# Gate and up projection in three 256-column passes, stationary operands moved by 64 bytes

## The chip, the cores and the metric

The kernel runs on one core of a Trainium2 chip. The metric is the device time of one execution in microseconds, given as the median of several runs. A profiled execution is taken besides; its trace has the start and the length of each engine's instructions.

## The reference

A trunk of two pre-norm layers over 256 tokens of width 1024, all in float32. Layer 0 mixes tokens by attention with a forget gate, layer 1 by block-sparse attention with a relative-position bias; with 256 tokens the one block of layer 1 is the whole sequence, so it is plain causal attention with a bias. Each layer ends with a SwiGLU feed-forward part and a gated embedding:

```python
def reference(...):
    h = x
    for i in range(DEPTH):                       # DEPTH = 2
        u = _rmsnorm(h, attn_norm_g[i])
        proj = u @ w_in                          # q, k, v (layer 0: and the forget gates)
        h = h + _merge_heads(attention(q, k, v)) @ w_o
        u = _rmsnorm(h, ffn_norm_g[i])
        gu = u @ ffn_w_in[i]                     # D_FF = 2816 columns of gate, 2816 of up
        h = h + (jax.nn.silu(gu[..., :D_FF]) * gu[..., D_FF:]) @ ffn_w_out[i]
        gate = jax.nn.sigmoid(_rmsnorm(h, ple_norm_g[i]) @ ple_w_gate[i])
        h = h + gate * (p[i] @ ple_w_up[i])
    return _rmsnorm(h, final_norm_g)
```

## The kernel before

**Split products.** Every matrix product is made of three products of split operands, so that it comes near float32. An operand is written as a high part (`hi`, rounded to TensorE's float32r) and a low part (`lo`, what is left). `mm3` (line 72) accumulates hi*hi, hi*lo and lo*hi in PSUM. In a call `mm(o, a, b)` the operand `a` is stationary: TensorE loads it as weights of 128 columns, a LDWEIGHTS in the profile, before each matmul. The operand `b` is moving: its columns stream through, up to 512 in a pass.

**Weights.** The host packs all weights into tiles of 128 x 1024 in the order of use. `half()` (line 106) fetches the next one by SP's queue into `raw`, ScalarE copies it into `whi` (line 119), and VectorE subtracts to give `wlo` (line 120). There are six buffers of each. `blocks()` (line 123) is the same tile seen as eight stationary blocks of 128 columns.

**Where weights move and where they stand still.** In the products of v, the output projection wo, the down projection fo, the gate pg and the embedding pu, the tokens are stationary and 512 columns of weights move (`tokens`, line 221). In the query and key projections pq (`project`, line 356) the weights are stationary, 128 columns for one block of features, and the 256 tokens move; the norm's result `g` is held in eight blocks of hi and lo, 256 columns each and next to each other (`Norm.both`, line 133). In the attention's values po (`values`, line 418) slices of `vhi` and `vlo` are stationary and the 256 columns of transposed probabilities move. `vhi` and `vlo` are tiles of 128 x 8 x 192 (line 211).

**Gate and up.** `up` (line 466) makes one block of 128 features of gate (a = 0) and of up (a = 1) for each `f` of 22. Here the kernel uses two passes for the three products: `whi` against hi and lo side by side, 512 columns into one whole bank (line 473), then `wlo` against hi, 256 columns, added to the bank's left half (line 475). The bank's right half so holds hi*lo. `gated` (line 497) copies the right half out on ScalarE (line 502), adds the left half on VectorE (503), multiplies by the row of norm factors (504), takes SiLU on ScalarE and the product with up on VectorE, and splits the result for the down projection `fo`. The first two blocks (`f` = 0 and 1) are interleaved by `k`, since the norm's second half is transposed in their midst; from then on each round makes two blocks of gate and up, then 24 passes of `fo` for the two blocks before.

**Order.** Each engine runs its instructions in the program's order. PSUM has eight banks; one pool of eight tiles rotates over them. Buffers are released by semaphores that the tile framework sets. In the built program all operands of matmuls begin at a multiple of 256 bytes in their partition, but for three kinds: the 16-column weights of the forget gate (`fh` and `fl`, 64 bytes apart), the bias table (`rl`), and the broadcast columns `col`.

Of the kernel before, what the change touches and what calls it, by code (L numbers as in the profile page):

```python
# [28 lines left out]
F32R = mybir.dt.float32r  # L29
AF = mybir.ActivationFunctionType  # L30
ALU = mybir.AluOpType

P = 128
S = 256
D = 1024
KT = D // P
H = 16
DH = 64
NP = H // 2
# [7 lines left out]
HW = 1024  # L47
# [4 lines left out]
RVW = 384  # L52


@with_exitstack
def trunk(ctx: ExitStack, tc: tile.TileContext, x, xt, pt, w, wf, cst, gains, gf, bf, rel, hot, rvm, out):
    nc = tc.nc
    one = ctx.enter_context(tc.tile_pool(name="one", bufs=1))
    work = ctx.enter_context(tc.tile_pool(name="work", bufs=2))
# [4 lines left out]
    def bank(name):  # L64
        return ps.tile([P, 512], F32, tag="bank", name=name)

    def f32(ap):
        return ap.bitcast(F32)

    mm = nc.tensor.matmul  # L70

    def mm3(o, a, b, start, stop):
        (ah, al), (bh, bl) = a, b
        mm(o, ah, bh, start=start, stop=False, skip_group_check=True)  # L74
        mm(o, ah, bl, start=False, stop=False, skip_group_check=True)  # L75
        mm(o, al, bh, start=False, stop=stop, skip_group_check=True)  # L76
# [26 lines left out]

    state = {"next": 0}

    def half():

        i = state["next"]
        state["next"] += 1
        raw = work.tile([P, HW], F32, tag="raw", bufs=RAW, name=f"raw{i}")  # L110
        hi = work.tile([P, HW], F32R, tag="whi", bufs=6, name=f"whi{i}")
        lo = work.tile([P, HW], F32R, tag="wlo", bufs=6, name=f"wlo{i}")
        parts = 2 if i < 2 else 1
        for q in range(parts):
            c = slice(q * HW // parts, (q + 1) * HW // parts)
            if i == 0 and q == 1:
                nc.sync.dma_start(hx[:, 1], xt[:, 1])
            nc.sync.dma_start(raw[:, c], w[i][:, c])
            nc.scalar.activation(hi[:, c], raw[:, c], AF.Copy)  # L119
            nc.vector.tensor_tensor(lo[:, c], raw[:, c], f32(hi[:, c]), op=ALU.subtract)  # L120
        return hi, lo

    def blocks():

        return [t.rearrange("p (k c) -> p k c", k=KT) for t in half()]


    class Norm:
# [51 lines left out]

    nm = Norm(0)
    first = [half()]
    nm.block(0, hx[:, 0])
    nm.block(1, hx[:, 1])
    first.append(half())
    for b in range(1, 4):
        nc.sync.dma_start(hx[:, 2 * b:2 * b + 2], xt[:, 2 * b:2 * b + 2])
# [20 lines left out]
    nc.gpsimd.memset(nhalf, -0.5)  # L208
    zero = one.tile([H, S], F32, name="zero")
    nc.gpsimd.memset(zero, 0.0)  # L210
    vhi = one.tile([P, NP, 192], F32R, name="vhi")
    vlo = one.tile([P, NP, 192], F32R, name="vlo")
    vf = one.tile([P, NP, 192], F32, name="vf")
    for t in (f32(vhi), f32(vlo), vf):
        nc.gpsimd.memset(t[:, :, DH:2 * DH], 0.0)
# [1 line left out]
    def split(hi, lo, src):  # L217
        nc.scalar.activation(hi, src, AF.Copy)
        nc.vector.tensor_tensor(lo, src, f32(hi), op=ALU.subtract)

    def tokens(o, x, t, w, start, stop):

        at = slice(t * P, (t + 1) * P)
        mm3(o, (x[0][:, at], x[1][:, at]), w, start, stop)
# [10 lines left out]
    def residual(hf, bks):  # L235
        for t in range(2):
            at = h[:, t, hf * HC:(hf + 1) * HC]
            nc.vector.tensor_tensor(at, at, bks[t], op=ALU.add)
# [67 lines left out]
    def attention(layer, nm, mid, early, nf):  # L306
# [49 lines left out]
        def project(j, a):  # L356
            hi, lo = blocks()
            if a == 0:
                pq[j] = bank(f"pq{layer}_{j}")
            bk = pq[j]  # L360
            for k in range(KT):
                mm3(bk[:, a * S:(a + 1) * S], (hi[:, k], lo[:, k]), nm.k(k),
                    start=(k == 0), stop=(k == KT - 1))
            if a == 0:
                return
            del pq[j]
            t = work.tile([P, 2, S], F32, tag="qkt", name=f"qkt{layer}_{j}")
            nc.vector.tensor_tensor(t.rearrange("p a s -> p (a s)"), bk,
                                    nm.row.rearrange("p a s -> p (a s)"), op=ALU.mult)
            th = work.tile([P, 2, S], F32R, tag="qkh", name=f"qkh{layer}_{j}")  # L370
            tl = work.tile([P, 2, S], F32R, tag="qkl", name=f"qkl{layer}_{j}")
            split(th, tl, t)
            qk[j] = t, th, tl
# [88 lines left out]
    def ffn(layer, nm, filler, np_):  # L462
        acc = []
        prod = {}

        def up(fs):

            bks = {(f, a): bank(f"gu{layer}_{f}_{a}") for f in fs for a in range(2)}

            def step(f, a, wt, k):  # L470
                hi, lo = wt
                b = bks[f, a]
                mm(b, hi[:, k], nm.both[:, k].rearrange("p a s -> p (a s)"), start=(k == 0), stop=False,  # L473
                   skip_group_check=True)
                mm(b[:, 0:S], lo[:, k], nm.hi[:, k], start=False, stop=(k == KT - 1), skip_group_check=True)  # L475

            if fs[0] == 0:
                wts = {f: (blocks(), blocks()) for f in fs}
                for k in range(KT):
                    if k == 3:  # L480
                        nm.turn(1)
                        nm.square(1)
                    for f in fs:
                        for a in range(2):
                            step(f, a, wts[f][a], k)
                nm.root()
                return fs, bks
            for a in range(2):
                wt = blocks()
                for k in range(KT):  # L490
                    step(fs[0], a, wt, k)
                if fs[0] == 2 and a == 0:
                    nm.spread()
                    gated(*early)
            gated(fs, bks)

        def gated(fs, bks):
            for f in fs:
                t = work.tile([P, 2, S], F32, tag="t2k", bufs=3, name=f"gut{layer}_{f}")
                for a in range(2):  # L500
                    b = bks[f, a]
                    nc.scalar.activation(t[:, a], b[:, S:2 * S], AF.Copy)  # L502
                    nc.vector.tensor_tensor(t[:, a], t[:, a], b[:, 0:S], op=ALU.add)  # L503
                nc.vector.tensor_tensor(t, t, nm.row, op=ALU.mult)  # L504
                sg = work.tile([P, S], F32, tag="sg", name=f"sg{layer}_{f}")
                nc.scalar.activation(sg, t[:, 0], AF.Silu)
                nc.vector.tensor_tensor(sg, sg, t[:, 1], op=ALU.mult)
                th = work.tile([P, S], F32R, tag="th", bufs=4, name=f"fh{layer}_{f}")
                tl = work.tile([P, S], F32R, tag="tl", bufs=4, name=f"fl{layer}_{f}")
                split(th, tl, sg)  # L510
                prod[f] = th, tl

        def down(f, wt):
            hi, lo = wt
            for t in range(2):
                for hf in range(2):
                    cols = slice(hf * HC, (hf + 1) * HC)
                    tokens(acc[hf][t], prod[f], t, (hi[:, cols], lo[:, cols]), f == 0, False)

        def last(f, hf):  # L520

            wt = half()
            for i in range(2):
                for t in range(2):
                    tokens(acc[hf][t], prod[f + i], t, [w[:, i * HC:(i + 1) * HC] for w in wt],
                           False, f + i == FT - 1)

        early = up([0, 1])
        acc.extend([bank(f"fo{layer}_{hf}_{t}") for t in range(2)] for hf in range(2))
        for f in range(2, FT, 2):  # L530
            up([f])
            up([f + 1])
            if f == FT - 6:
                pp = filler()
            if f < FT - 2:
                down(f - 2, half())
                down(f - 1, half())
        last(FT - 4, 0)
        filler(pp)
        last(FT - 2, 0)  # L540
        residual(0, acc[0])
        last(FT - 4, 1)
        np_.turn(0)
        np_.square(0)
        last(FT - 2, 1)
        residual(1, acc[1])
# [83 lines left out]
    for layer in range(2):  # L630
# [8 lines left out]
        nm = Norm(3) if layer == 0 else None  # L639
# [95 lines left out]
```

## Time and profile before

| | |
|---|---|
| median of 3 runs | 684.88 us (684.73 to 684.99) |
| the profiled execution's own time | 686.33 us |
| its span, first to last instruction | 684.6 us |
| mean granted TensorE clock | 0.993 |

How to read the profile: PE is TensorE's matmuls and PEld its weight loads; they overlap. DVE is VectorE, ACT ScalarE, POOL GpSimd. A row of a group has line, engine, operation, output<-inputs, shapes and count, then busy time in us and the mean of one in ns, then the engine's idle time before them and what ended it. A row of the timeline has the start in us, the length in us, the engine, line, operation and shape, and how many in a row were merged. A matmul's length includes the time to drain the array, which overlaps the next matmul, so the distance of two starts is what a pass costs. The chain is the work that ended last, followed back from the end. The profile calls all operands f32 or fp32r by their width.

### The profile page before, as it was taken

The numbers are of one execution on the slowest core, as the hardware profiler recorded it, in microseconds if no ns is written. First come the engines' busy times: TensorE is split into PE (matmuls) and PEld (weight loads), VectorE is DVE, ScalarE is ACT, GpSimd is POOL, SyncE is SP. The second block draws the span as 40 slices with busy tenths as digits, with TensorE's granted clock in tenths as the row PEclk, the third lists the DMA queues.
The fourth block names the chain that finished last, engine by engine and source line by source line (L and its number), as shares of the span: only waits on it lengthen the run. The fifth ranks groups of instructions, "written<-read, shape, count | busy, mean of one in ns | idle before, by whom it ended". The sixth has DMA issues, their size and how long they took to land.

```text
span 684.6 us, 10549 instructions
## 1 busy us (share of the span) xinstructions
PE 668.7 (98%) x3876; PEld 580.1 (85%) x3876; DVE 478.4 (70%) x868; ACT 411.2 (60%) x786; POOL 29.4 (4%) x55
## 2 busy tenths in 40 slices
PE   8999999999999999999999999999999999999994
PEld 6798998888888888888889999888888888888883
DVE  4688886678666666766676788766866666676673
ACT  6876665575555555557665766656655555555663
POOL 1066000000000000000000000000000000000000
PEclk9999999999999999999999999999999999999998
DMA  7989333446655555555586533343665555565401
GB/s 267 376 287 350 124 124 124 154 150 225 190 195 189 189 186 199 186 185 185 182 282 197 168 125 124 110 168 109 238 209 184 184 185 189 185 208 191 164 1 62
DMA packets 37524, 125.81 MB, mean 184 GB/s; under 512 B 4240, under 2 KB 7008, under 8 KB 37472
## 3 DMA queue, kind: packets, MB, share of 16 engines
q1 hardware_dynamic: 36016, 121.35, 52.5%
q0 software_dynamic: 608, 2.11, 0.9%
q10 hardware_dynamic: 848, 1.68, 0.7%
q8 instruction: 30, 0.49, 0.3%
q14 instruction: 22, 0.18, 0.1%
HBM read 124.03 MB, written 4.24 MB: 187 GB/s over the span
## 4 chain that ended last, share of the span: by engine, by line
PE 94%; DMA 2%; ACT 1%; issue 1%; DVE 1%; SPq 0%; POOLq 0%; POOL 0%; DVEq 0%; ACTq 0%
PE gu L473 24%; PE gu L475 12%; PE fo L74 6%; PE fo L76 6%; PE fo L75 6%; PE pq L74 5%; PE pq L75 5%; PE pq L76 5%; PE wo L76 2%; PE wo L74 2%; PE wo L75 2%; PE pg L76 2%; PE pg L74 2%; PE pg L75 2%; PE pp L410 2%; PE v L76 2%
## 5 line engine op out<-in xcount | busy, mean ns | idle before, releaser
L120 DVE TENSOR_TENSOR wlo<-raw,whi 128x1024 fp32r<-128x1024 f32 (+1 forms) x218 | 264.8, 1218 | 169.2 <-ACT whi L119 167.8
L119 ACT ACTIVATE whi<-raw 128x1024 fp32r<-128x1024 f32 (+1 forms) x218 | 228.4, 1051 | 195.3 <-issue 67.6
L473 PE MATMUL gu<-g,whi 128*128 128x512 f32 x704 | 249.4, 398 | 0.0
L475 PE MATMUL gu<-g,wlo 128*128 128x256 f32 x704 | 197.5, 281 | 0.0
L473 PEld LDWEIGHTS gu<-g,whi 128*128 128x128 f32 x704 | 132.2, 188 | 32.4
L475 PEld LDWEIGHTS gu<-g,wlo 128*128 128x128 f32 x704 | 132.9, 189 | 0.7
L74 PE MATMUL pq<-g,whi 128*128 128x256 f32 x256 | 75.3, 294 | 0.0
L75 PE MATMUL pq<-g,whi 128*128 128x256 f32 x256 | 73.0, 285 | 0.0
L76 PE MATMUL pq<-g,wlo 128*128 128x256 f32 x256 | 72.9, 285 | 0.0
L74 PE MATMUL fo<-whi,fh 128*128 128x512 f32 x176 | 69.3, 394 | 0.0
L76 PE MATMUL fo<-whi,fl 128*128 128x512 f32 x176 | 68.8, 391 | 0.0
L75 PE MATMUL fo<-wlo,fh 128*128 128x512 f32 x176 | 68.6, 390 | 0.0
L74 PEld LDWEIGHTS pq<-g,whi 128*128 128x128 f32 x256 | 49.7, 194 | 0.9 <-ACT whi L119 0.6
L75 PEld LDWEIGHTS pq<-g,whi 128*128 128x128 f32 x256 | 49.7, 194 | 0.0
L76 PEld LDWEIGHTS pq<-g,wlo 128*128 128x128 f32 x256 | 49.6, 194 | 0.0
L76 PEld LDWEIGHTS fo<-whi,fl 128*128 128x128 f32 x176 | 33.0, 188 | 7.5
L74 PEld LDWEIGHTS fo<-whi,fh 128*128 128x128 f32 x176 | 33.0, 188 | 7.1
L75 PEld LDWEIGHTS fo<-wlo,fh 128*128 128x128 f32 x176 | 33.1, 188 | 6.3
L503 DVE TENSOR_TENSOR gut<-gut,gu 128x256 f32<-128x256 f32 x88 | 36.1, 416 | 0.5 <-ACT gut L502 0.5
L502 ACT ACTIVATE gut<-gu 128x256 f32<-128x256 f32 x88 | 31.8, 369 | 0.0
L394 ACT ACTIVATE e<-e,mn 128x128 f32<-128x128 f32 x64 | 28.3, 444 | 5.7 <-DVE mn L391 5.5
L504 DVE TENSOR_TENSOR gut<-gut,row 128x512 f32<-128x512 f32 x44 | 30.2, 691 | 1.2
(134 smaller groups left out, 909.2 us busy)
## 6 DMA issues: line engine op xcount, KB each, us to landing
raw<-w SPq DMA_DIRECT2D x214, 512.0 KB, 3.3
d<-d SPq DMA_DIRECT2D x4, 768.0 KB, 12.8
bias<-cd POOLq DMA_DIRECT2D x4, 512.0 KB, 8.7
bias<-d SPq DMA_DIRECT2D x4, 512.0 KB, 6.2
raw<-w SPq DMA_DIRECT2D x4, 256.0 KB, 5.3
h<-x ACTq DMA_DIRECT2D x2, 512.0 KB, 5.7
hx<-xt SPq DMA_DIRECT2D x3, 256.0 KB, 5.8
p<-pt SPq DMA_DIRECT2D x2, 256.0 KB, 3.8
```

What stands on the lines that cost most here:

```text
L74: mm(o, ah, bh, start=start, stop=False, skip_group_check=True)
L75: mm(o, ah, bl, start=False, stop=False, skip_group_check=True)
L76: mm(o, al, bh, start=False, stop=stop, skip_group_check=True)
L119: nc.scalar.activation(hi[:, c], raw[:, c], AF.Copy)
L120: nc.vector.tensor_tensor(lo[:, c], raw[:, c], f32(hi[:, c]), op=ALU.subtract)
L394: nc.scalar.activation(e[:, sl[q]], e[:, sl[q]], AF.Exp, scale=-1.0, bias=mn[:, q:q + 1], accum_out=mn[:, 2 + q:3 + q])
L410: nc.tensor.transpose(pp[:, q * P:(q + 1) * P], e[:, q * P:(q + 1) * P], ident)
L473: mm(b, hi[:, k], nm.both[:, k].rearrange("p a s -> p (a s)"), start=(k == 0), stop=False, skip_group_check=True)
L475: mm(b[:, 0:S], lo[:, k], nm.hi[:, k], start=False, stop=(k == KT - 1), skip_group_check=True)
L502: nc.scalar.activation(t[:, a], b[:, S:2 * S], AF.Copy)
L503: nc.vector.tensor_tensor(t[:, a], t[:, a], b[:, 0:S], op=ALU.add)
L504: nc.vector.tensor_tensor(t, t, nm.row, op=ALU.mult)
```

## The change

Stationary weights (pq, gate and up) and v now begin 64 bytes past a multiple of 256 bytes; the tiles are 256 bytes longer for it. Weights that move stay at a multiple of 256. Gate and up are made by `mm3`, three passes of 256 columns, into the left and the right half of one bank, and `gated` multiplies the bank by the row factors at once.

```diff
+LINE = 64
+APART = 16
...
-    def half():
+    def half(at=0):
...
-        hi = work.tile([P, HW], F32R, tag="whi", bufs=6, name=f"whi{i}")
-        lo = work.tile([P, HW], F32R, tag="wlo", bufs=6, name=f"wlo{i}")
+        hi, lo = (work.tile([P, HW + LINE], F32R, tag=n, bufs=6, name=f"{n}{i}")[:, at:at + HW] for n in ("whi", "wlo"))
...
-        return [t.rearrange("p (k c) -> p k c", k=KT) for t in half()]
+        return [t.rearrange("p (k c) -> p k c", k=KT) for t in half(APART)]
...
-    vhi = one.tile([P, NP, 192], F32R, name="vhi")
-    vlo = one.tile([P, NP, 192], F32R, name="vlo")
+    vhi, vlo = (one.tile([P, NP * 192 + LINE], F32R, name=n)[:, APART:APART + NP * 192].rearrange("p (j c) -> p j c", j=NP)
+                for n in ("vhi", "vlo"))
...
-            bks = {(f, a): bank(f"gu{layer}_{f}_{a}") for f in fs for a in range(2)}
-
-            def step(f, a, wt, k):
-                hi, lo = wt
-                b = bks[f, a]
-                mm(b, hi[:, k], nm.both[:, k].rearrange("p a s -> p (a s)"), start=(k == 0), stop=False,
-                   skip_group_check=True)
-                mm(b[:, 0:S], lo[:, k], nm.hi[:, k], start=False, stop=(k == KT - 1), skip_group_check=True)
+            bks = {f: bank(f"gu{layer}_{f}") for f in fs}
+
+            def step(f, a, wt, k, start):
+                mm3(bks[f][:, a * S:(a + 1) * S], (wt[0][:, k], wt[1][:, k]), nm.k(k), start, k == KT - 1)
...
-                            step(f, a, wts[f][a], k)
+                            step(f, a, wts[f][a], k, k == 0 and a == 0)
...
-                    step(fs[0], a, wt, k)
+                    step(fs[0], a, wt, k, k == 0)
...
-                for a in range(2):
-                    b = bks[f, a]
-                    nc.scalar.activation(t[:, a], b[:, S:2 * S], AF.Copy)
-                    nc.vector.tensor_tensor(t[:, a], t[:, a], b[:, 0:S], op=ALU.add)
-                nc.vector.tensor_tensor(t, t, nm.row, op=ALU.mult)
+                nc.vector.tensor_tensor(t.rearrange("p a s -> p (a s)"), bks[f],
+                                        nm.row.rearrange("p a s -> p (a s)"), op=ALU.mult)
```

## The prediction

> **What bounds the kernel now.** I read the page first: busy shares, the granted clock and the chain that ended last.
>
> ```profile
> span 684.6 us, 10549 instructions
> ...
> PE 668.7 (98%) x3876; PEld 580.1 (85%) x3876; DVE 478.4 (70%) x868; ACT 411.2 (60%) x786; POOL 29.4 (4%) x55
> ...
> PEclk9999999999999999999999999999999999999998
> ...
> PE 94%; DMA 2%; ACT 1%; issue 1%; DVE 1%; SPq 0%; POOLq 0%; POOL 0%; DVEq 0%; ACTq 0%
> PE gu L473 24%; PE gu L475 12%; PE fo L74 6%; PE fo L76 6%; PE fo L75 6%; PE pq L74 5%; PE pq L75 5%; PE pq L76 5%; PE wo L76 2%; PE wo L74 2%; PE wo L75 2%; PE pg L76 2%; PE pg L74 2%; PE pg L75 2%; PE pp L410 2%; PE v L76 2%
> ```
>
> TensorE makes 94% of the chain at the full clock, so only the spacing of its passes counts. The busy time of a matmul overlaps the next one; I therefore take spacings from start times in the timeline. The groups give the counts:
>
> ```profile
> L473 PE MATMUL gu<-g,whi 128*128 128x512 f32 x704 | 249.4, 398 | 0.0
> L475 PE MATMUL gu<-g,wlo 128*128 128x256 f32 x704 | 197.5, 281 | 0.0
> L74 PE MATMUL pq<-g,whi 128*128 128x256 f32 x256 | 75.3, 294 | 0.0
> L74 PE MATMUL po<-th,vhi 128*128 128x256 f32 x32 | 9.3, 289 | 0.0
> ```
>
> Query/key projections (pq) are 3 x 256 = 768 passes of 256 columns, the values (po) 3 x 32 = 96 more. One undisturbed stretch of pq, first and last of 24 passes:
>
> ```profile
> 47.86 0.28 PE L74 MATMUL pq<-g,whi 128*128 128x256 f32 x1
> ...
> 50.62 0.28 PE L76 MATMUL pq<-g,wlo 128*128 128x256 f32 x1
> ```
>
> 2.76 us over 23 steps: 120 ns a pass. The down projection (fo), 512 columns a pass, 12 steps:
>
> ```profile
> 206.43 0.39 PE L74 MATMUL fo<-whi,fh 128*128 128x512 f32 x1
> ...
> 209.15 0.39 PE L473 MATMUL gu<-g,whi 128*128 128x512 f32 x1
> ```
>
> 2.72 / 12 = 226.7 ns. The 256 extra columns cost 106.7 ns, so 256 columns alone are worth 106.7 ns, and each pass carries **13.3 ns that its columns don't explain**. Gate and up (gu) alternate a pass of 512 and one of 256:
>
> ```profile
> 209.15 0.39 PE L473 MATMUL gu<-g,whi 128*128 128x512 f32 x1
> 209.38 0.28 PE L475 MATMUL gu<-g,wlo 128*128 128x256 f32 x1
> 209.49 0.40 PE L473 MATMUL gu<-g,whi 128*128 128x512 f32 x1
> 209.72 0.28 PE L475 MATMUL gu<-g,wlo 128*128 128x256 f32 x1
> 209.84 0.40 PE L473 MATMUL gu<-g,whi 128*128 128x512 f32 x1
> 210.08 0.28 PE L475 MATMUL gu<-g,wlo 128*128 128x256 f32 x1
> 210.20 0.40 PE L473 MATMUL gu<-g,whi 128*128 128x512 f32 x1
> ...
> 220.44 0.40 PE L74 MATMUL fo<-whi,fh 128*128 128x512 f32 x1
> ```
>
> 32 pairs in 11.29 us: 352.8 ns a pair, 16.4 ns over the columns' 320.0 for each of its two passes. The starts repeat every three pairs (1.05 to 1.06 us) and not every pair. Yet the same instructions hold another rhythm earlier, 16 pairs in 5.55 us, 346.9 ns:
>
> ```profile
> 147.74 0.39 PE L473 MATMUL gu<-g,whi 128*128 128x512 f32 x1
> ...
> 153.29 0.39 PE L74 MATMUL fo<-whi,fh 128*128 128x512 f32 x1
> ```
>
> 704 x 352.8 = 248.4 us for gu, which is the 36% that the chain gives it.
>
> **What the excess is.** After a stall of PE the granted clock fell for about 3 us (the 0.98 of the stage from 35 us in the table further down), and ten pq passes ran so:
>
> ```profile
> 54.71 0.41 PE L76 MATMUL pq<-g,wlo 128*128 128x256 f32 x1
> ...
> 56.84 0.41 PE L74 MATMUL pq<-g,whi 128*128 128x256 f32 x1
> ```
>
> 213 ns a pass is twice 106.7, so the clock was at half, with nothing left over. A dead time fixed in ns would still be there, and one fixed in array cycles would have doubled. So the excess looks like two streams getting in each other's way at full rate: a pass's moving columns, and the load of the next pass's weights, which starts with it:
>
> ```profile
> 47.86 0.19 PEld L75 LDWEIGHTS pq<-g,whi 128*128 128x128 f32 x1
> ```
>
> That gu has two rhythms for the same work says the loss depends on how the two streams fall against each other. In the program every operand of these passes starts on a multiple of 256 bytes, so both streams start at the same place in the line; that is what the change shifts. Against it speaks the forget-gate product pf, whose weights are 16 columns and start 0, 64, 128 and 192 bytes into the line in turn:
>
> ```profile
> 20.86 0.28 PE L74 MATMUL pf<-g,fh 128*16 128x256 f32 x1
> ...
> 23.20 0.28 PE L76 MATMUL pf<-g,fl 128*16 128x256 f32 x1
> ```
>
> 2.34 us over 20 steps: 117 ns throughout, with no step that follows the offset. But those loads read one 64-byte piece, against eight, and the passes sit below the 120.
>
> The floor of a weight load of 128 columns shows where the moving side is short, in eight transposes (128 columns each):
>
> ```profile
> 133.75 1.03 PE L148 MATMUL tp<-ident,h 128*128 128x128 f32 x8
> ...
> L148 PE MATMUL tp<-ident,h 128*128 128x128 f32 x80 | 10.4, 272 | 0.0
> ```
>
> (1.03 - 0.27) / 7 = 109 ns from one to the next. No pass with new weights can be expected under that.
>
> **The change part by part.** *The shift of stationary operands.* It touches the weights of gu and pq and the v operands of po. fo, wo, pg and v keep their places, so their 226.7 ns stays. Call the new spacing of a 256-column pass X. No row shows a full load shifted against its moving operand. Its lower bound is the load's 109. For the upper, two streams that stay in step hold 120; a gu pass of 512 shows more, up to 0.24 us (209.84 to 210.08), 26.7 ns over its columns, hence 133. I take **X = 112**, nearest to the 256-column steps of 0.11 to 0.12 in the gu rows (209.38 to 209.49), a little over the floor. 864 passes x (120 - 112) = 6.9 us gained; at 109, 9.5; at 120, nothing; at 133, 11.2 lost.
>
> *Gate and up in three 256-column passes.* 704 pairs become 2,112 passes, with one weight load more a pair. New cost 704 x 3 x 112 = 236.5 us against 248.4: 11.9 us gained; at 109 it is 230.2 (18.2 gained); at 120 it is 253.4 (5.0 lost); at 133 it is 280.9 (32.5 lost). Note that by itself this edit loses at today's spacing.
>
> *One bank and a shorter gate.* Removed: a copy and an addition for each half. The row product now reads the bank, for which qkt is the nearest row:
>
> ```profile
> L502 ACT ACTIVATE gut<-gu 128x256 f32<-128x256 f32 x88 | 31.8, 369 | 0.0
> L503 DVE TENSOR_TENSOR gut<-gut,gu 128x256 f32<-128x256 f32 x88 | 36.1, 416 | 0.5 <-ACT gut L502 0.5
> L504 DVE TENSOR_TENSOR gut<-gut,row 128x512 f32<-128x512 f32 x44 | 30.2, 691 | 1.2
> L368 DVE TENSOR_TENSOR qkt<-pq,row 128x512 f32<-128x512 f32 x16 | 10.8, 677 | 2.5 <-PE pq L76 2.5
> ```
>
> ScalarE loses 31.8 us, VectorE 36.1 + 44 x 0.014 = 36.7. PE waited for neither (its idle is 0.0 in the gu rows), so this is worth 0 on the path: TensorE's own queue hides it. It would be worth something only if VectorE came to bind. The instruction order on each engine is otherwise that of before, with gu blocks of 48 passes where 32 stood; no DMA is added or moved.
>
> *Can the feeders keep up?* By stage:
>
> ```profile
> 35.00:106.00 71.00, 69.50 (x576) 66.36 (x576) 59.01 (x158) 47.98 (x126) 22.20 (x37) 0.98 0.61 215
> 165.00:310.00 145.00, 145.00 (x759) 123.45 (x758) 100.44 (x142) 77.20 (x125) 0.00 (x0) 1.00 0.58 193
> 369.00:436.00 67.00, 67.00 (x573) 64.22 (x573) 53.52 (x154) 46.23 (x121) 0.00 (x0) 1.00 0.44 141
> ```
>
> Columns after the length are PE, PEld, DVE, ACT, POOL, clock, DMA share, GB/s. Attention has some 430 of the 864 passes per layer, so it shrinks by 3.5 us: VectorE goes from 59.0 of 71 to 59.0 of 67.5 (87%) in layer 0, where it already made PE wait once for 1.5 us. In the feed-forward stretch it gets lighter, and 193 GB/s rises by a few per cent, under the 215 of the first attention. I take nothing off; the range holds a microsecond or two of stall.
>
> *Sum.* 6.9 + 11.9 = 18.8 us. The profiled execution took 686.33 us for a span of 684.60 (1.73 around it), hence 667.5 for such an execution; the three unprofiled runs have a median of 684.88, 1.45 lower, hence **666**.
>
> The Trainium skill gives a warm gap of N/2.4 + 2.5 ns (TensorE: Matmul & The Clock Gate, Back-to-back issue gap); for 256 columns that is 109.2 ns, by which the sum would be 27 us gained, 658. The measured 120 and 226.7 lie 11 ns above it.
>
> **The rivals.** *The shift does nothing* (the other side). The 13.3 ns belongs to the exchange of weights, not to addresses. Then X stays 120, the pairs go from 352.8 to 360, and the time is 684.88 + 5.0 = **690**. For it: pf's 117 at four offsets. Against it: the half-clock passes without excess, and two rhythms for one instruction sequence. It decides from X = (248.4 + 103.7) us / 2,976 passes = 118.3 ns on: any smaller relief loses. The same page (What happens when you issue a matmul) speaks for this rival: "Loading the next tile's weights doesn't steal SBUF read bandwidth from the running matmul." By that rule no offset can help; the trace agrees as far as pf goes and disagrees in the half-clock passes.
>
> *The shift hurts.* The load of 512 bytes now touches three 256-byte stretches instead of two, or the streams lock one step worse: X = 127 to 133, 2,976 x (127 - 118.3) = 26 us or more lost, **711** and up. Nothing in the profile speaks for it but the 26.7 ns of single gu passes.
>
> *A part of it goes.* The passes move to pf's 117: 704 x (352.8 - 351) + 864 x 3 = 3.9 us gained, **681**.
>
> *All of it goes.* X = 109: 27.7 us gained, **657**.
>
> **How the numbers follow.** Forecast with X from 109 to 115: 0.52, its own range 657 to 675. Partial relief: 0.08. Break-even within 0.2% (1.4 us, about what a measurement here can tell from none): 0.04. Nothing: 0.27. Harm: 0.09. Faster is 0.52 + 0.08 = 0.60, same 0.04, slower 0.36. The range reaches from full relief, 657, to the first rival with a little stall, 692; harm is left out.
>
> **What would show it.** Right: pq and gu passes 110 to 115 ns apart in the timeline, gu blocks of 96 passes in some 10.8 us where 11.29 stood, fo unchanged at 226.7, and VectorE's idle in gu longer. Wrong: pq still at 120 (the shift is nothing), weight loads or passes beyond 125 (harm), or PE idle before sp with VectorE as the releaser (the feeder binds).

## The result, and the profile after

The changed kernel takes **683.58 us** (median of 20 runs, 682.1 to 685.1) against 684.91 us for the kernel before (20 runs, 684.31 to 687.71): a ratio of 0.9974, 95% interval 0.9966 to 0.9983. It is faster, as forecast, but by 1.3 us (1.8 by the ratio) and not by 18.8; the time lies inside the range of 657 to 692 and far from the 666 that stood in it.

The page of the changed kernel, its busy shares, the clock and the groups of gate and up:

```profile
span 682.0 us, 11771 instructions
...
PE 666.4 (98%) x4580; PEld 611.0 (90%) x4580; DVE 452.5 (66%) x780; ACT 385.9 (57%) x698; POOL 29.1 (4%) x55
...
PEclk9998999999999999999999999999999999999997
...
L78 PE MATMUL gu<-g,whi 128*128 128x256 f32 x704 | 198.2, 281 | 0.0
L80 PE MATMUL gu<-g,wlo 128*128 128x256 f32 x704 | 197.8, 281 | 0.0
L79 PE MATMUL gu<-g,whi 128*128 128x256 f32 x704 | 197.8, 281 | 0.0
...
L499 DVE TENSOR_TENSOR gut<-gu,row 128x512 f32<-128x512 f32 x44 | 30.0, 689 | 18.0 <-PE gu L80 18.0
```

TensorE is as full as before, at the same mean clock (0.992 against 0.993); the 704 added passes are there. VectorE (478.4 to 452.5 us) and ScalarE (411.2 to 385.9 us) have become lighter, and VectorE now waits 18.0 us for gate and up: the relief shows up as waiting, as it must on an engine that doesn't set the end.

Where the 1.3 us came from is read by the starts of stages. Timeline rows of the kernel before (first pass of gu and of pg in layer 0, of pq and of wo in layer 1):

```profile
129.52 0.40 PE L473 MATMUL gu<-g,whi 128*128 128x512 f32 x1
...
321.68 0.39 PE L74 MATMUL pg<-whi,g 128*128 128x512 f32 x1
...
368.31 0.36 PE L74 MATMUL pq<-g,whi 128*128 128x256 f32 x1
...
432.57 0.47 PE L74 MATMUL wo<-whi,o 128*128 128x512 f32 x1
```

and the same four of the changed kernel:

```profile
128.12 0.28 PE L78 MATMUL gu<-g,whi 128*128 128x256 f32 x1
...
320.25 0.39 PE L78 MATMUL pg<-whi,g 128*128 128x512 f32 x1
...
366.88 0.37 PE L78 MATMUL pq<-g,whi 128*128 128x256 f32 x1
...
430.04 0.47 PE L78 MATMUL wo<-whi,o 128*128 128x512 f32 x1
```

The feed-forward stage took 192.16 us and takes 192.13: **gate and up gave nothing**. Layer 1's attention took 64.26 us and takes 63.16: 1.1 us came from there. Layer 0's attention, with the fall of the clock in it, took 67.38 us and takes 66.80 (from the first pq pass at 35.29 and 34.52 to the first wo pass at 102.67 and 101.32). One round of gu and fo shows why. Timeline of the changed kernel, the first pass of 96 of gu, then of 24 of fo, then the next round:

```profile
157.51 0.28 PE L78 MATMUL gu<-g,whi 128*128 128x256 f32 x1
...
168.82 0.40 PE L78 MATMUL fo<-whi,fh 128*128 128x512 f32 x1
...
174.29 0.28 PE L78 MATMUL gu<-g,whi 128*128 128x256 f32 x1
```

11.31 us over 96 passes is **117.8 ns a pass**, where 32 pairs took 11.29 us before; all 18 rounds between two blocks of fo are alike. The query and key projections show two spacings. Rows of the changed kernel, an early block of 24 passes (first and last), and 23 passes of a late one:

```profile
47.00 0.28 PE L78 MATMUL pq<-g,whi 128*128 128x256 f32 x1
...
49.61 0.28 PE L80 MATMUL pq<-g,wlo 128*128 128x256 f32 x1
...
92.47 0.28 PE L79 MATMUL pq<-g,whi 128*128 128x256 f32 x1
...
95.06 0.28 PE L80 MATMUL pq<-g,wlo 128*128 128x256 f32 x1
```

2.61 / 23 = 113.5 ns, and 2.59 / 22 = 117.7 ns: the same instruction, the same offset, two rhythms, neither of them the 120 of before.

### The profile page after: what moved, and what is told of

Read it like the earlier page. It is cut to its first block, busy times and chain, and to the rows that moved or that the text cites. A ratio compares the mean times of both kernels' runs of the same rounds, so it can differ in the third digit from the quotient of the medians.

```text
span 682.0 us, 11771 instructions
## 1 busy us (share of the span) xinstructions
PE 666.4 (98%) x4580; PEld 611.0 (90%) x4580; DVE 452.5 (66%) x780; ACT 385.9 (57%) x698; POOL 29.1 (4%) x55
## 4 chain that ended last, share of the span: by engine, by line
PE 90%; issue 1%; DVE 0%; ACT 0%; POOLq 0%; POOL 0%; ACTq 0%
PE gu L80 12%; PE gu L78 12%; PE gu L79 12%; PE fo L78 6%; PE fo L79 6%; PE fo L80 6%; PE pq L78 4%; PE pq L79 4%; PE pq L80 4%; PE wo L78 2%; PE wo L80 2%; PE wo L79 2%; PE pg L80 2%; PE pg L78 2%; PE pg L79 2%; PE pp L413 2%
## 5 line engine op out<-in xcount | busy, mean ns | idle before, releaser
L78 PE MATMUL gu<-g,whi 128*128 128x256 f32 x704 | 198.2, 281 | 0.0
L79 PE MATMUL gu<-g,whi 128*128 128x256 f32 x704 | 197.8, 281 | 0.0
L79 PEld LDWEIGHTS gu<-g,whi 128*128 128x128 f32 x704 | 134.7, 191 | 0.7
L78 PEld LDWEIGHTS gu<-g,whi 128*128 128x128 f32 x704 | 132.4, 188 | 0.8
L78 PE MATMUL pq<-g,whi 128*128 128x256 f32 x256 | 74.5, 291 | 0.0
L79 PE MATMUL pq<-g,whi 128*128 128x256 f32 x256 | 72.2, 282 | 0.0
L221 ACT ACTIVATE fh<-sg 128x256 fp32r<-128x256 f32 x44 | 18.1, 415 | 47.5 <-DVE sg L503 47.5
L499 DVE TENSOR_TENSOR gut<-gu,row 128x512 f32<-128x512 f32 x44 | 30.0, 689 | 18.0 <-PE gu L80 18.0
```

Source lines behind the costliest of these rows:

```text
L499: nc.vector.tensor_tensor(t.rearrange("p a s -> p (a s)"), bks[f], nm.row.rearrange("p a s -> p (a s)"), op=ALU.mult)
```

## The experiments

Two questions were open: is it the offset that moves the spacing, and why 117.8 in one place and 113 in another. Each kernel is compared with the kernel before, which ran beside it on the same chip. From chip to chip the median of the kernel before went from 684.91 to 685.45 us, so a difference between two of the experiments, or between one and the changed kernel's 683.58, is good to about half a microsecond.

### The shift alone

The 64 bytes, with gate and up left in passes of 512 and 256 columns.

```diff
-        return [t.rearrange("p (k c) -> p k c", k=KT) for t in half()]
+        return [t.rearrange("p (k c) -> p k c", k=KT) for t in half(APART)]
```

> The kernel before with the 64-byte shift of stationary weights and v alone; gate and up keep their pairs of 512 and 256 columns in two banks. Theory A (the shift eases a contention whose size depends on how the load of weights falls against the moving columns): pq passes 113 to 118 ns apart as in the changed kernel, 864 passes x 2 to 6 ns = 2 to 5 us gained there; the gu pairs go from 352.8 ns to about 348, another 3 us gained; about 678 to 681 us. Theory B (the shift does nothing, and the gain of the changed kernel is from the passes or from the lighter gate): pq at 120 ns, pairs at 352.8 ns, 684.9 us. Theory C (the shift is of use to passes of 256 columns alone): pq 113 to 118, pairs still 352.8 ns, 680 to 683 us.

685.08 us (12 runs) against 685.45; ratio 0.9987 (0.9974 to 1.0). The timeline of this kernel, 16 pairs of gu up to fo:

```profile
163.80 0.40 PE L476 MATMUL gu<-g,whi 128*128 128x512 f32 x1
...
169.45 0.40 PE L78 MATMUL fo<-whi,fh 128*128 128x512 f32 x1
```

5.65 / 16 = 353.1 ns a pair, as before (352.8). A pair of 512 and 256 columns gains nothing from the 64 bytes. The passes of pq did move: layer 1's attention took 63.24 us in this trace, where 64.26 stood. But each feed-forward stage took 0.2 us more (192.37 against 192.16). So the spacings are those of theory C, and the time is not: it is theory B's 684.9.

### The passes alone

The changed kernel with the distance set back to 0.

```diff
-APART = 16
+APART = 0
```

> The changed kernel without the shift: all stationary operands at a multiple of 256 bytes, gate and up in three passes of 256 columns into one bank. Theory A: gu and pq passes stay in step at 120 ns, gu costs 704 x 360 = 253.4 us against 248.4, about 690 us. Theory B: as the changed kernel, passes of 118 ns and about 683.6 us.

689.09 us (6 runs, 688.81 to 690.05) against 685.45; ratio 1.0045 (1.0029 to 1.0061). The timeline of this kernel, first of 96 passes of gu and the first of fo:

```profile
157.28 0.28 PE L78 MATMUL gu<-g,whi 128*128 128x256 f32 x1
...
168.79 0.40 PE L78 MATMUL fo<-whi,fh 128*128 128x512 f32 x1
```

11.51 / 96 = 119.9 ns. Against the kernel before it this is 3.6 us lost, where the first rival of the prediction said 5. The changed kernel gained 1.3, so with the three passes the shift is worth 3.64 + 1.33 = 5.0 us. At 64 bytes neither half of the change gains by itself (the shift alone 0.4 us, its interval reaching to none); together they come out a little ahead.

### TensorE alone, many offsets

A kernel with only TensorE working: stationary and moving operands lie in SBUF, runs of 48 passes of 256 columns cycle through them at a given distance, behind six passes of 512 columns (`a`) or behind transposes (`b`). The trunk is left out, and x is returned.

```diff
+    def narrow(name, off, cols, n=48, moff=0):
+        for i in range(n):
+            w = stt[:, 1 if j == 2 else 0, o + k * 128:o + k * 128 + cols]
+            mm(b[:cols, 0:S], w, mvt[:, c:c + S], start=(i == 0), stop=(i == n - 1), skip_group_check=True)
```

> TensorE alone, on operands that are loaded once; the trunk is left out and x is returned. Runs of 48 passes of 256 columns with 128 stationary columns that begin 0, 16, 32, 48, 64, 96, 128, 160, 192 and 224 bytes past a multiple of 256, each entered three ways (behind passes of 512 columns, behind four transposes, behind a product of two 128-column passes); then passes of 512 columns at 0, 64 and 128, loads of 16, 32 and 64 columns, and moving operands shifted by 64 and 128 bytes. Theory A: 120 ns at 0, 113 to 118 at 64, and a spacing that changes with the offset and with the entry; 512 columns go from 226.7 to about 220 when shifted. Theory B: 120 ns at every offset. If VectorE, ScalarE and the DMAs of the kernel make the excess (theory D), every run here comes near 109.

The timeline of this kernel. `n64a` has the stationary operand 64 bytes off, `w` rows have 512 columns a pass, `c16` and `c32` have 16 and 32 stationary columns at offset 0, `m64u0` has the moving operand alone 64 bytes off, and `m64u64` both:

```profile
18.11 5.92 PE L55 MATMUL n0a<-mv,stt 128*128 128x256 f32 x48
...
82.28 6.14 PE L55 MATMUL n48b<-mv,stt 128*128 128x256 f32 x48
...
95.73 5.82 PE L55 MATMUL n64a<-mv,stt 128*128 128x256 f32 x48
...
101.74 5.71 PE L55 MATMUL n64b<-mv,stt 128*128 128x256 f32 x48
...
192.08 5.77 PE L55 MATMUL n224a<-mv,stt 128*128 128x256 f32 x48
...
209.78 5.61 PE L62 MATMUL w0y<-mv,stt 128*128 128x512 f32 x24
215.23 5.76 PE L62 MATMUL w64y<-mv,stt 128*128 128x512 f32 x24
...
227.76 5.76 PE L55 MATMUL c16u0z<-mv,stt 128*16 128x256 f32 x48
...
234.75 5.61 PE L55 MATMUL c32u0z<-mv,stt 128*32 128x256 f32 x48
...
255.51 5.82 PE L55 MATMUL m64u0a<-mv,stt 128*128 128x256 f32 x48
...
268.65 5.91 PE L55 MATMUL m64u64a<-mv,stt 128*128 128x256 f32 x48
```

The spacing is (length - 0.28) / 47, for 512 columns (length - 0.39) / 23. At offset 0 it is 120.0 ns; at 64 bytes 117.9 behind passes of 512 columns. Behind transposes the first step takes some 0.2 us, and the other 46 average (5.71 - 0.28 - 0.20) / 46 = 113.7. At 224 bytes it is 116.8, and at 48 bytes behind transposes (6.14 - 0.28 - 0.20) / 46 = 123.0. With both operands moved it is back at 119.8, and with the moving operand alone moved by 64 bytes it is 117.9, as with the weights at 192 (117.8): only their distance within 256 bytes counts. For 512 columns 0 is better: 227.0 against 233.5. All this is with the other engines idle (VectorE is busy for 0.1 us of this kernel's span, ScalarE for 7.2 at its start): gate, memory traffic and PSUM readers have no part in it. Theory A's 220 ns for shifted passes of 512 columns did not come. With 32 stationary columns the spacing at offset 0 is 113.4, with 16 it is 116.6, against 120.0 with 128: the length of the weight load counts too, but the shortest is not the fastest.

### One transpose ahead of each round

If the way a run of passes is entered picks its rhythm, something between fo and gu should move it.

```diff
+            if fs[0] % 2 == 0:
+                nc.tensor.transpose(bks[fs[0]][:, 0:P], ident, ident)
```

> The changed kernel with one transpose of the identity (128 columns, overwritten at once) ahead of each round of gate and up. In the changed kernel pq passes run 113.3 ns apart in some stretches and 117.8 in others, gu always 117.8; in the run with TensorE alone a shift of 64 bytes gave 117.8 behind 512-column passes and 113.3 behind transposes. Theory A (two rhythms for the same passes, and how the run is entered picks one): gu passes at 113.3 ns, 22 rounds x (96 x 4.5 - 110) ns = 7 us gained on the changed kernel, about 677 us. Rival (gu's 117.8 comes from what goes on beside it, DMA and VectorE work of the feed-forward stage, and the entry is of no matter): gu stays at 117.8 and the transposes cost 22 x 0.11 = 2.4 us, about 686 us.

682.49 us (6 runs) against 685.37; ratio 0.9956 (0.9939 to 0.9973). Two rounds in this kernel's timeline, each from the second pass of gu to the first of fo:

```profile
173.82 0.28 PE L79 MATMUL gu<-g,whi 128*128 128x256 f32 x1
...
184.60 0.40 PE L78 MATMUL fo<-whi,fh 128*128 128x512 f32 x1
...
190.31 0.28 PE L79 MATMUL gu<-g,whi 128*128 128x256 f32 x1
...
201.50 0.40 PE L78 MATMUL fo<-whi,fh 128*128 128x512 f32 x1
```

10.78 / 95 = 113.5 ns in the one, 11.19 / 95 = 117.8 in the other, with the same instructions and the same entry. Of the 18 rounds behind fo 8 ran at 113.5 and 10 at 117.8, in the same order in both layers: the entry matters, but one transpose does not settle it.

### Entries compared, more offsets

TensorE alone again: at 64 bytes with different single passes as the entry (behind 512-column passes each time), and finer offsets.

```diff
+        wide(f"w{i}z", 0, 6)
+        one_pass(f"b{i}z", *arg)
+        narrow(f"e{i}z", 64, 128)
```

> TensorE alone, trunk left out. Passes of 256 columns at offsets 8, 56, 72, 80, 88, 112, 144, 176, 208 and 240 bytes, entered from 512-column passes and from one transpose; passes of 512 columns at 16, 32, 48, 96, 160, 192, 208, 224 and 240; and at 64 bytes nine ways of entry (one or two transposes, one pass of other sizes), then 24 passes of 512 columns and 24 passes of 256 again. Theory A: spacings between 113 and 123 that depend on offset and entry; 512 columns nowhere under 226.7 or only a little, as 0 was the best of 0, 64 and 128; at 64 bytes one transpose gives 113.3 like four, and the 512-column passes in between throw it back to 117.8. Rival (spacing set by the offset alone): the nine entries all give one value.

The timeline of this kernel: 88 bytes behind 512-column passes and behind one transpose; then 64 bytes behind one transpose (`e0z`), behind two (`e1z`), and behind one pass of 256 columns whose stationary operand is at offset 0 (`e7z`); then 24 passes at 64 bytes after 24 passes of 512 columns at offset 0 (`g7z`); last, 64 bytes behind one pass of 512 columns that is itself at 64 bytes (`e8z`):

```profile
68.17 5.63 PE L55 MATMUL n88a<-mv,stt 128*128 128x256 f32 x48
...
73.67 5.85 PE L55 MATMUL n88b<-mv,stt 128*128 128x256 f32 x48
...
196.35 5.71 PE L55 MATMUL e0z<-mv,stt 128*128 128x256 f32 x48
...
211.73 5.90 PE L55 MATMUL e1z<-mv,stt 128*128 128x256 f32 x48
...
303.90 5.60 PE L55 MATMUL e7z<-mv,stt 128*128 128x256 f32 x48
...
314.81 2.99 PE L55 MATMUL g7z<-mv,stt 128*128 128x256 f32 x24
...
319.26 5.61 PE L55 MATMUL e8z<-mv,stt 128*128 128x256 f32 x48
```

`e7z` holds (5.60 - 0.28) / 47 = 113.2 from its first step. `e0z` reaches it after a few steps, `e1z` stays at (5.90 - 0.28 - 0.20) / 46 = 117.8. Straight behind passes of 512 columns at offset 0 it is (2.99 - 0.28) / 23 = 117.8, which is just how each round of gu follows fo. One pass of 512 columns at 64 bytes in between gives (5.61 - 0.28) / 47 = 113.4. Of the nine entries six end at 113.3 and three at 117.8: two transposes, one pass of 128 columns with weights at offset 0, and one of 256 columns with 32 stationary columns. The rival, one value for all, is out; no rule that sorts the nine was found.

At 88 bytes, straight behind passes of 512 columns, it is (5.63 - 0.28) / 47 = 113.8. Among the 20 distances of the two runs 88 bytes stands alone there: it ends at 113.3, 8 bytes at 115.5, 208 and 224 at 116.7, and the other sixteen at 117.3 to 120.1 (means of the last 20 steps). Passes of 512 columns came under the 226.7 ns of distance 0 at none of the distances tried. Two ways out followed from this, and both were tried in the whole kernel.

### 88 bytes

```diff
-APART = 16
+APART = 22
```

> The changed kernel with 88 bytes in place of 64 as the distance of the stationary operands. Theory R (the spacing is set by the offset and by how the run is entered; the product alone on TensorE held 113.3 ns at 88 bytes behind passes of 512 columns and 116.7 behind transposes): gu falls from 117.8 to 113.3 ns, 2,112 x 4.5 ns = 9.5 us less, pq at 113 to 117, so some 674 us (672 to 678). Theory F (in the kernel the other engines, their reads and writes of SBUF and PSUM, hold gu near 118 whatever the offset): gu stays at 117 to 119, 682 to 686 us.

**674.25 us** (4 runs, 673.97 to 675.82) against 685.2; ratio 0.9842 (0.9823 to 0.9862). A round of gu in this kernel's timeline:

```profile
156.16 0.28 PE L78 MATMUL gu<-g,whi 128*128 128x256 f32 x1
...
167.06 0.40 PE L78 MATMUL fo<-whi,fh 128*128 128x512 f32 x1
```

10.90 / 96 = 113.5 ns. 22 floats are 88 bytes. One constant turns a change worth 1.3 us into one worth 11. Over the changed kernel 9.3 us came of the 9.5 expected, and that they agree so well is in part luck: from the starts of all passes gate and up give 8.3 (249.1 to 240.8 us), since the first two rounds of each layer, which are broken by transposes, run in part at 116.7. In the traced execution the clock also stayed up in layer 0's attention (granted 1.00 from 50 to 60 us, where the changed kernel's trace has 0.83).

### One pass at offset 0 ahead of each round

```diff
+            if fs[0] % 2 == 0:
+                mm(bks[fs[0]][:, 0:S], nm.hi[:, 0, 0:P], nm.hi[:, 0], start=True, stop=True)
```

> The changed kernel with one extra pass of 256 columns ahead of each round of gate and up, whose stationary operand is at a multiple of 256 bytes (its sum is overwritten by the first true pass). Theory R: behind such a pass the product alone held 113.3 ns from the first step on, so all 22 rounds go to 113.3: 22 x (96 x 4.5 - 114) ns = 7 us less than the changed kernel, 676 to 678 us. Theory F: gu stays at 117.8 and the extra passes cost 22 x 0.114 = 2.5 us, 685 to 687 us. If only some of the rounds move, as behind one transpose, the time lies between and the start of a round holds more than its entry pass.

676.81 us (4 runs, 676.54 to 677.75) against 685.2; ratio 0.9878 (0.9857 to 0.9898). A round of this kernel, from its first true pass:

```profile
156.64 0.28 PE L78 MATMUL gu<-g,whi 128*128 128x256 f32 x1
...
167.52 0.40 PE L78 MATMUL fo<-whi,fh 128*128 128x512 f32 x1
```

10.88 / 96 = 113.3 ns, at the 64 bytes of the changed kernel, and so in all 18 rounds behind fo. Ahead of the second round of each layer, which follows passes of gu that already run at 117.8, the extra pass changed nothing, so not all of the 22 rounds went over as expected. Work was *added*, and the kernel is 6.8 us faster than the changed one (gate and up 6.1 of it, 249.1 to 243.0 us): the 117.8 is a state that the run falls into, not the price of the pass.

### One short pass ahead of each round

The same with a pass of 128 columns and the round's own weights, not in the first round.

```diff
+                if a == 0 and fs[0] % 2 == 0:
+                    mm(bks[fs[0]][:, 0:P], wt[0][:, 0], nm.hi[:, 0, 0:P], start=True, stop=True)
```

> As the run before, but the extra pass has 128 columns and the round's own weights at 64 bytes, and the first round (two blocks interleaved) has none. Theory R: 113.3 ns behind it as in the product alone: 20 rounds x (96 x 4.5 - 60) ns = 7.4 us less than the changed kernel, 675 to 677 us. Theory F: 1.2 us more than the changed kernel, 684 to 686 us.

678.07 us (4 runs) against 685.2; ratio 0.9894 (0.9878 to 0.991): 5.5 us less than the changed kernel, where 7.4 were expected. A round in this kernel's timeline, from the short pass on:

```profile
157.43 0.22 PE L490 MATMUL gu<-g,whi 128*128 128x128 f32 x1
...
168.44 0.40 PE L78 MATMUL fo<-whi,fh 128*128 128x512 f32 x1
```

With the short pass's 0.06 us and one step of 0.17 us taken off, (11.01 - 0.06 - 0.17) / 95 = 113.5 ns. The expectation counted 20 rounds that gain 0.37 us each. The trace has 18 that take 11.01 us where 11.31 stood, 18 x 0.30 = 5.4 us: the first step behind the short pass takes 0.17 us instead of 0.11, and the second round of each layer, broken by transposes, falls back to 117.8.

### The old gate put back

88 copies on ScalarE and 88 additions on VectorE as before the change, in the changed kernel.

```diff
+                for a in range(2):
+                    nc.scalar.activation(t[:, a], bks[f][:, a * S:(a + 1) * S], AF.Copy)
+                    nc.vector.tensor_tensor(t[:, a], t[:, a], bks[f][:, 0:S], op=ALU.add)
```

> The changed kernel with the copies on ScalarE and the additions on VectorE put back into the gate, 88 of each, of the old shapes (their results are overwritten). Theory R (the spacing of TensorE's passes is all that counts, and the lighter gate was worth nothing): within 0.2% of the changed kernel, 682.5 to 685 us, the passes of gu at 117.8 as before. Rival G (the lighter gate paid for what was gained, by fewer reads of PSUM and SBUF beside TensorE): 1.5 to 5 us slower than the changed kernel, 685 to 689 us.

683.28 us (10 runs, 682.66 to 684.97), against the changed kernel's 683.58: nothing. The page of this kernel has the work back:

```profile
L500 ACT ACTIVATE gut<-gu 128x256 f32<-128x256 f32 x88 | 32.2, 371 | 24.3 <-DVE gut L501 24.3
L501 DVE TENSOR_TENSOR gut<-gut,gu 128x256 f32<-128x256 f32 x88 | 36.2, 415 | 8.2 <-ACT gut L500 8.1
```

68 us of work on two engines cost 0 on the path.

### 88 bytes with the old pairs

```diff
-APART = 16
+APART = 22
```

The edit is made in the kernel of the shift alone.

> The kernel before with the stationary operands moved by 88 bytes and gate and up left in passes of 512 and 256 columns. Theory R (the offset helps only where passes of 256 columns follow each other; one of 512 is best at 0): a pair stays at 350 to 355 ns, gu gains nothing, pq and po at some 117: 683 to 686 us. Rival (88 bytes are better for every pass): a pair at 226.7 + 113.3 = 340 ns, 704 x 12.8 = 9 us less, 673 to 676 us, and the three passes would not be needed.

682.02 us (7 runs, 680.63 to 683.97) against 685.32; ratio 0.9951 (0.9931 to 0.9971), a microsecond under the expected range. 16 pairs in this kernel's timeline:

```profile
163.23 0.39 PE L476 MATMUL gu<-g,whi 128*128 128x512 f32 x1
...
168.82 0.40 PE L78 MATMUL fo<-whi,fh 128*128 128x512 f32 x1
```

5.59 / 16 = 349.4 ns a pair against three passes of 113.5 = 340.5. The offset gives the pairs 3 ns; the rest needs passes of equal length. Still, the shift by 88 bytes alone gains 3.3 us, more than the whole change at 64: gate and up go from 248.4 to 246.7 us, and layer 1's attention from 64.26 to 62.95.

## Why the prediction was right and wrong

**What bounds the kernel: right.** The spacing of TensorE's passes gives the time of gate and up in every run, and 68 us of work put back on VectorE and ScalarE changed nothing.

**What the excess is: right in kind.** The spacing follows the distance of the two operands (120.0, 117.9, 116.8 ns at 0, 64 and 224 bytes with TensorE alone) and depends on the length of the weight load (113.4 with 32 columns at offset 0). The Trainium skill (TensorE: Matmul & The Clock Gate, What happens when you issue a matmul) says: "Loading the next tile's weights doesn't steal SBUF read bandwidth from the running matmul." For float32r passes these runs speak against it: moving the weights' address alone moves the rate of the passes. Whether it is a port, a bank or something else of SBUF is not shown.

**The evidence of pf: misread.** Its 117 at four offsets was set against the idea. But with 16 stationary columns a pass is 116.6 even at offset 0: the number belonged to the short load and said nothing of loads of 128 columns.

**The step that failed: X = 112.** The prediction took one spacing for all 256-column passes, "nearest to the 256-column steps of 0.11 to 0.12 in the gu rows", over a floor of 109 from transposes. Measured is 117.8 in gu. The term of gate and up, 11.9 us, becomes 248.4 - 704 x 3 x 117.8 ns = -0.4 us; from the starts of all passes it is -0.7 (248.4 to 249.1). The term of pq and po, 6.9 us, was 1.1 us in layer 1 and 0.6 in layer 0's attention, since most blocks of pq run at 117.7 and only some at 113.5. The rows that the prediction read did not say 112: the three steps shown are 0.11, 0.12 and 0.12 us, 117 ns on average. And the 109 of the transposes was no floor that passes of 256 columns come near: the lowest steady spacing that any offset or entry gave is 113.3. That the sign came out right is owed to the smaller term, not to the one that was to bring most.

**What the step overlooked.** The prediction saw two rhythms of the same gu instructions in the kernel before, and took them as a sign that addresses matter. They were a sign of more: at one offset there can be several stable rhythms, and the entry picks one. Behind fo it is 117.8 at 64 bytes, in all 18 rounds; behind six of the nine entries tried at that offset it is 113.3. The forecast should have carried two values of X, one for each entry.

**The break-even held.** 118.3 was worked out as the spacing above which the change loses. At 117.8 it gains, little; at 119.9, without the shift, it lost: 689.09 where the first rival gave 690. That rival fell with the shift's 5.0 us. What came lies at the edge of "break-even within 0.2%" (0.19% by the medians, 0.26% by the ratio), which had a chance of 0.04. "A part of it goes" (117, 681 us; 0.08) had the spacing of gu nearly right. "All of it" and "the shift hurts" fell.

**Terms at zero.** The gate: 0, shown by putting it back. The feeders: gu waited for nothing (idle 0.0 in its rows). fo: 24 passes take 5.47 us (168.82 to 174.29), where 5.50 stood (203.65 to 209.15 in the kernel before); over all blocks that is 0.7 us (121.1 to 120.4), which makes up for what gate and up lost.

**What stays open.** Why some entries bring 113.3 and others not, and one transpose ahead of a round now the one and now the other; why 88 bytes are good behind 512 columns and worse behind a transpose ((5.85 - 0.28 - 0.20) / 46 = 116.7), and where the two streams meet.

## What to carry to other kernels

When a stream of equal instructions runs a few per cent over what its size explains, measure the stream alone with the address distance of its operands, the length of its passes and the work ahead of it as variables before changing the kernel: here such a run gave 88 bytes (674.25 us), where 64 had been worth 1.3 us. Look for more than one steady spacing of the same instruction in the old trace: then the entry counts, and a forecast needs a value for each. Passes of different length want different distances (here 0 for 512 columns, 88 bytes for 256 behind them), so a distance is set for each kind of operand by itself.

## What the runs showed of the hardware

- The spacing of float32r passes of 256 columns with 128-column weights ran from 113.3 to 123.0 ns by the distance of stationary and moving operand and by the entry; 512 columns took 227.0 ns at 0 and 233.5 at 64 bytes.
- At 64 bytes two rhythms, 117.8 and 113.3, each hold for a whole round of 96 passes; behind passes of 512 columns an extra pass of 114 ns at offset 0 brings the second in place of the first (11.31 us a round to 10.99 with the extra pass), and in the midst of passes at 117.8 it does not.
- The Trainium skill (TensorE: Matmul & The Clock Gate, Back-to-back issue gap) gives N/2.4 + 2.5 ns as the gap of the isolated matmul, 109.2 for 256 columns, and says that in a stream with weight loads both operations set the spacing. No steady run of such passes reached the 109.2: the lowest, 113.3, is 4.1 over it.
